# Diagonal inverses of a recurrence substituted in 16x16 blocks and joined to 32x32 by a level of small TensorE products

## The chip, the core and the metric

The kernel runs on one core of one Trainium2 chip. The metric is the device time of one execution in microseconds (us), the median of several runs. The engines are TensorE (PE in the profile; its weight loads are PEld), VectorE (DVE), ScalarE (ACT), GpSimd (POOL) and SyncE (SP), which issues DMAs here. A line such as L698 is a line of the kernel before; the lines of the changed kernel stand higher, by 4 ahead of the changed functions and by 33 behind them (L698 becomes L731).

## What is computed

One inference step of a one-layer decoder trunk over 576 tokens (a prompt of 512 and 8 samples of 8 tokens), width 1024. A combined projection feeds two head groups; their outputs go through an output projection, a SwiGLU and a gated embedding. The change lies in the second group, 16 heads of width 64 whose state follows a delta rule:

```python
def step(s, inp):
    r_t, w_t, k_t, v_t, kk_t, a_t = inp
    s_kk = jnp.einsum('bhvk,bhk->bhv', s, kk_t)
    s = (s * w_t[:, :, None, :] - s_kk[..., None] * (kk_t * a_t)[:, :, None, :]
         + v_t[..., None] * k_t[:, :, None, :])
    return s, jnp.einsum('bhvk,bhk->bhv', s, r_t)
```

The kernel takes it in chunks of 64 tokens. Inside a chunk the steps depend on each other through a triangular 64x64 matrix I + L for each head, and the kernel needs its inverse. There are 9 chunks (8 of the prompt, one holding the samples), 16 heads.

## The kernel before

**Fills.** The projections run as `fill`s: one fill makes 128 columns of the projection for all 576 tokens, as 48 TensorE products of 128x288 (L221, L222, L223 in `mm3`; an input and a weight are each split into two parts, and three of the four products are made). Weights are loaded (`raw`), rounded on ScalarE (`whi`, through the helper at L93) and their rest taken on GpSimd or VectorE (`wlo`, L206). The program calls a stated number of fills at stated places (`fill_at`, `fill_for`), and a scheduler then sets the order on each engine, within what tiles and pools allow. In what follows "a fill" as a count is one such TensorE product.

**Quarters.** The 16 heads go in four quarters of four heads (q = 0 to 3; two pairs jj of two heads e). For a quarter: its projections (`fill_for`), `prep` (decays, normalised keys, scaled operands), `start_states`, `gram` (L613, the products between tokens of a chunk, masked into `Lst`, which holds L), `bonus` (L246) and `decayed`; then `inverse`, which is `solve`, some fills, and `combine`; then `chain` and `head_norm`.

**solve (L652).** A 64x64 matrix is taken as 2x2 blocks of 32. The two diagonal blocks (z = 0, 1) of all heads and chunks are 72 blocks of 32x32, which four DMAs and a load bring to 72 partitions, one block to each (`L`). VectorE starts from I - L and runs 30 steps of substitution on whole blocks: step jx multiplies (L674) and subtracts (L676) jx·(31 - jx) elements in each partition. A transposed copy of the 36 blocks with z = 0 (L677) overwrites L. Td (the inverses) and Ad (the transposed ones) go to DRAM.

**combine (L681).** Td and Ad are loaded into `TT` and `AA`, block by block to the partitions e·64 + z·32. Then 32 products of 32x32 (L698; each is two instructions in the trace) into one PSUM tile, an eviction with the sign turned (L705 on VectorE and a ScalarE one), 32 more products (L712) and an eviction (L719 and ScalarE) that puts the off-diagonal blocks into TT.

**chain (L739).** Steps 1, then the samples (0), then 2 to 8, each step over TensorE, ScalarE and VectorE: L789, an eviction `xs` (L792), the product with the inverse (L797), L802, an eviction (L805), L823 and the state's update (L831), and L812 beside it. `marks` only notes instructions for other places.

**What orders the work here.** The PSUM pool `cx` (two tiles, taken in turn) serves combine, chain and head_norm, so a quarter's combine starts its products behind the head norm of the quarter before. The chain of a quarter runs beside the preparation of the next one. For quarter 3, whose inverse is called late, the preparation of the other head group follows directly: a load of dt (L997, on SyncE's queue, behind the stores of head_norm, L917), a running sum on VectorE (L1020 to L1043), an exponential on ScalarE, and 15 transposes of 16 columns on TensorE (L1037).

## Time and profile before

| | |
|---|---|
| three runs | 1345.02, 1345.34, 1348.39 us; median 1345.34 |
| span of the profiled execution | 1349.0 us |
| mean granted TensorE clock | 0.940 |
| busy: PE, DVE, ACT, POOL | 1246.8, 826.0, 618.9, 625.6 us |
| L674 and L676 together, 240 operations | 94.4 us of VectorE |

The profile is of one execution, which is not one of the three runs. Busy times are sums over the whole span. The stretch from 146 to 600 us holds the inverses of the four quarters and the chains of the first three; ahead of it lie loading, the first projections and quarter 0's preparation, behind it quarter 3's chain beside the rest of the trunk. A granted clock of 1 is full speed.

### The profile page before, as it was taken

What the parts mean: (1) busy time and instruction counts of PE and PEld (TensorE: products, weight loads), DVE (VectorE), ACT (ScalarE), POOL (GpSimd) and SP (SyncE); (2) the same over time, 40 slices, a digit from 0 to 9 for tenths busy, and PEclk for the clock granted to TensorE, in tenths of its full rate; (3) what the DMA queues carried; (4) which work ended last, traced back from release to release, by engine and by line L of the source; (5) the groups of instructions that cost most, each with busy time, mean ns of one, the idle gap of its engine ahead of it and who ended that gap; (6) DMA issues with size and microseconds to landing.
All of it is one profiled execution on the core that took longest, in us unless ns stands there. A gap on an engine that the chain in (4) does not pass through costs nothing.

```text
span 1349.0 us, 26596 instructions
## 1 busy us (share of the span) xinstructions
PE 1246.8 (92%) x10525; PEld 1150.7 (85%) x10525; DVE 826.0 (61%) x1443; ACT 618.9 (46%) x1256; POOL 625.6 (46%) x597
## 2 busy tenths in 40 slices
PE   6897999999989978899999969989999999999997
PEld 6787897889868957788779859889999999999997
DVE  6648666887687785943466667886553135443454
ACT  6565436534654463343434364464442124433363
POOL 5425413642355154122456645565654336654642
PEclk9897799899979978889989989998999999999998
DMA  5322242234232412262454542222323222314322
GB/s 164 125 68 66 77 117 63 85 103 116 75 99 78 109 41 80 94 214 83 157 176 131 179 125 72 73 93 88 92 88 87 79 86 82 93 59 149 96 89 71
DMA packets 94461, 135.58 MB, mean 100 GB/s; under 512 B 34705, under 2 KB 39057, under 8 KB 94337
## 3 DMA queue, kind: packets, MB, share of 16 engines
q1 hardware_dynamic: 93760, 133.36, 32.4%
q8 instruction: 83, 1.36, 0.4%
q10 hardware_dynamic: 576, 0.52, 0.1%
q14 instruction: 42, 0.34, 0.1%
HBM read 106.10 MB, written 27.75 MB: 99 GB/s over the span
## 4 chain that ended last, share of the span: by engine, by line
PE 63%; DVE 14%; ACT 4%; issue 4%; DMA 3%; POOL 3%; DVEq 0%; SPq 0%; ACTq 0%; POOLq 0%
PE lin L234 21%; PE lin L1403 8%; PE lin L223 6%; PE lin L221 6%; PE lin L222 6%; DVE h L395 2%; PE lin L1508 1%; PE lin L1509 1%; PE lin L1510 1%; DVE tmp L674 1%; DVE wlo L206 1%; DVE Tt L676 1%; PE lin L613 1%; PE cx L797 1%; DVE suv L831 1%
## 5 line engine op out<-in xcount | busy, mean ns | idle before, releaser
L206 POOL TENSOR_TENSOR wlo<-raw,whi 128x512 fp32r<-128x512 f32 (+1 forms) x108 | 146.4, 1356 | 352.5 <-ACT whi L93 269.5
L93 ACT ACTIVATE whi<-raw 128x512 fp32r<-128x512 f32 (+1 forms) x232 | 143.3, 618 | 259.1 <-PE lin L234 126.4
L221 PE MATMUL lin<-xhi,whi 128*128 128x288 f32 (+1 forms) x784 | 243.3, 311 | 2.5 <-ACT whi L93 2.2
L223 PE MATMUL lin<-xhi,wlo 128*128 128x288 f32 (+1 forms) x784 | 241.5, 308 | 2.3 <-POOL wlo L206 2.3
L222 PE MATMUL lin<-xlo,whi 128*128 128x288 f32 (+1 forms) x784 | 241.5, 308 | 0.3 <-POOL xlo L194 0.3
L206 DVE TENSOR_TENSOR wlo<-raw,whi 128x512 fp32r<-128x512 f32 (+1 forms) x124 | 100.9, 814 | 103.2 <-PE lin L234 60.4
L221 PEld LDWEIGHTS lin<-xhi,whi 128*128 128x128 f32 (+1 forms) x784 | 151.0, 193 | 9.3 <-ACT whi L93 2.6
L223 PEld LDWEIGHTS lin<-xhi,wlo 128*128 128x128 f32 (+1 forms) x784 | 150.7, 192 | 6.2 <-POOL wlo L206 2.8
L222 PEld LDWEIGHTS lin<-xlo,whi 128*128 128x128 f32 (+1 forms) x784 | 150.8, 192 | 4.8 <-issue 1.2
L234 PE MATMUL lin<-xhi,whi 128*128 128x288 f32 x384 | 62.3, 297 | 3.2 <-ACT xhi L93 3.0
L234 PE MATMUL lin<-xlo,whi 128*128 128x288 f32 x384 | 60.8, 298 | 0.0
L234 PE MATMUL lin<-xhi,wlo 128*128 128x288 f32 x384 | 59.3, 297 | 0.0
L234 PEld LDWEIGHTS lin<-xhi,whi 128*128 128x128 f32 x384 | 54.6, 189 | 3.8 <-ACT xhi L93 1.7
L234 PEld LDWEIGHTS lin<-xlo,whi 128*128 128x128 f32 x384 | 54.8, 191 | 0.0
L234 PE MATMUL lin<-ah,wlo 128*128 128x288 f32 x352 | 54.7, 296 | 0.0
L234 PE MATMUL lin<-al,whi 128*128 128x288 f32 x352 | 54.7, 296 | 0.0
L234 PE MATMUL lin<-ah,whi 128*128 128x288 f32 x352 | 54.7, 296 | 0.0
L234 PEld LDWEIGHTS lin<-xhi,wlo 128*128 128x128 f32 x384 | 54.3, 191 | 0.0
L1403 PE MATMUL lin<-T,wh 128*128 128x288 f32 x320 | 50.1, 296 | 4.5 <-DVE T L194 2.8
L674 DVE TENSOR_TENSOR tmp<-L,Tt 72x30 f32<-72x30 f32 (+14 forms) x120 | 49.2, 410 | 3.2
L234 PEld LDWEIGHTS lin<-ah,whi 128*128 128x128 f32 x352 | 49.6, 189 | 0.0
L234 PEld LDWEIGHTS lin<-ah,wlo 128*128 128x128 f32 x352 | 49.6, 189 | 0.0
(425 smaller groups left out, 3197.8 us busy)
## 6 DMA issues: line engine op xcount, KB each, us to landing
raw<-wts SPq DMA_DIRECT2D x271, 256.0 KB, 2.6
S<-s_wkv SPq DMA_DIRECT2D x8, 512.0 KB, 5.1
hd<-s_ssm SPq DMA_DIRECT2D x8, 512.0 KB, 4.5
o_ssm_s<-hd SPq DMA_DIRECT2D x8, 512.0 KB, 2.9
xbc_d<-E SPq DMA_DIRECT2D x12, 288.0 KB, 2.1
x<-xT SPq DMA_DIRECT2D x8, 288.0 KB
gate_d<-g SPq DMA_DIRECT2D x8, 288.0 KB, 2.5
bv_d<-rw SPq DMA_DIRECT2D x8, 288.0 KB
```

Source lines behind the costliest of these rows:

```text
L93: return S.activation(out, in_, func, bias=bias, scale=scale)
L206: eng.tensor_tensor(lo[:, 0:n], raw[:, 0:n], hi[:, 0:n].bitcast(F32), ALU.subtract)
L221: T.matmul(ps[:, a:b], whi, xhi[:, a:b], start=first, stop=False)
L222: T.matmul(ps[:, a:b], whi, xlo[:, a:b], start=False, stop=False)
L223: T.matmul(ps[:, a:b], wlo, xhi[:, a:b], start=False, stop=last)
L234: T.matmul(ps[:, a:e], (hi, lo)[p][:, i * P:(i + 1) * P], xs[k + i][q][:, a:e], start=n == k + i == 0, stop=n == 2 and k + i == nk - 1, sk ...
L395: V.scalar_tensor_tensor(h[:], E[:, i:i + 600], w(i), h[:], ALU.mult, ALU.add)
L613: T.matmul(ps[:, c:c + 128].rearrange("p (a t) -> p a t", a=2), s.BK[jj][H[e], g].rearrange("p a t -> p (a t)"), s.G[H[e], g, jj, :, e], s ...
L674: V.tensor_tensor(o, L[:, jx:jx + 1, jx + 1:32].to_broadcast([NB, jx, n]), Tt[:, 0:jx, jx:jx + 1].to_broadcast([NB, jx, n]), ALU.mult)
L676: V.tensor_tensor(Tt[:, 0:jx, jx + 1:32], Tt[:, 0:jx, jx + 1:32], o, ALU.subtract)
L797: T.matmul(uw[H[e], jj, :], TT[H[e], g, jj, :], xs[H[e], jj, :], start=True, stop=True)
L1403: T.matmul(ps, (hi, lo)[p][:, k * P:(k + 1) * P], OPS[n][k][q], start=first and p == q == k == 0, stop=p == 1 and k == 3, skip_group_check ...
```

## The change

A diagonal block of 32x32 is now split once more, into two corners of 16x16 and an off-diagonal block of 16x16. VectorE substitutes both corners of all 72 blocks at once: 14 steps, step jx on 2·jx·(15 - jx) elements in each partition. `Tt` is one tile, cleared once at the start of the program, so the elements outside the corners stay zero; ScalarE writes the negated corners into it. The transposed copy is made by ScalarE, for all 72 blocks, so Ad is twice as long and four loads bring AA in place of two.

`combine` gets a level ahead of the old one. 64 products (L707) multiply L with the inverses' first corner in AA, in the four strips of 32 partitions, into one PSUM tile. VectorE evicts them with a factor per partition, `half`, which is -1 on the second 16 partitions of each 32 and 0 on the first. Then 64 products of 16x16 (L716) and 32 of 32x16 (L719, for z = 0 alone) into the two halves of another PSUM tile; VectorE adds the latter to AA (L723, two operations) and ScalarE copies the former into TT (L724, four copies). The old level follows as it was (L731, L745).

```diff
@@ -453,6 +453,10 @@
     H = (slice(0, 64), slice(64, 128))
     jj2 = (0, 1)
 
+    half = const("half", [P, 1])
+    V.tensor_reduce(half[:], ident[:].rearrange("p (q y k) -> p q y k", q=4, y=2)[:, :, 1, :], AX.XY, ALU.add, negate=True)
+    Tt = s2.tile([72, 1056], F32, tag="Tt", name=nm("Tt"))
+    G.memset(Tt[:], 0.0)
     inverses = []
     for i in range(2):
         TT = (se, sp)[i].tile([P, 9, 2, 64], F32, tag=f"TT{i}", name=f"TT{i}")
@@ -654,29 +658,34 @@
         q = s.q
         Ld = dp.tile([2, 2, 18, 32, 32], F32, tag=f"Ld{q}", name=f"Ld{q}")
         s.Td = dp.tile([2, 2, 18, 32, 32], F32, tag=f"Td{q}", name=f"Td{q}")
-        s.Ad = dp.tile([2, 18, 32, 32], F32, tag=f"Ad{q}", name=f"Ad{q}")
+        s.Ad = dp.tile([2, 2, 18, 32, 32], F32, tag=f"Ad{q}", name=f"Ad{q}")
         NB = 72
         for z in range(2):
             for e in range(2):
                 r0 = e * 64 + z * 32
                 nc.sync.dma_start(Ld[z, e].rearrange("g s t -> s g t"),
                                   s.Lst[r0:r0 + 32, :, :, z * 32:z * 32 + 32].rearrange("s g j t -> s (g j) t"))
-        L = sp.tile([NB, 32, 32], F32, tag="L", name=nm("L"))
-        nc.sync.dma_start(L[:], Ld[:].rearrange("z e g s t -> (z e g) s t"))
-        Tt = s2.tile([NB, 32, 32], F32, tag="Tt", name=nm("Tt"))
-        V.tensor_scalar(Tt[:], L[:], -1.0, None, ALU.mult)
-        V.tensor_tensor(Tt[:].rearrange("p s t -> p (s t)")[:, 0:1024:33],
-                        Tt[:].rearrange("p s t -> p (s t)")[:, 0:1024:33], ones[0:NB, 0:32], ALU.add)
-        tmp = s2.tile([NB, 256], F32, tag="tmp", name=nm("tmp"))
-        for jx in range(1, 31):
-            n = 31 - jx
-            o = tmp[:, 0:jx * n].rearrange("p (s t) -> p s t", s=jx)
-            V.tensor_tensor(o, L[:, jx:jx + 1, jx + 1:32].to_broadcast([NB, jx, n]),
-                            Tt[:, 0:jx, jx:jx + 1].to_broadcast([NB, jx, n]), ALU.mult)
-            V.tensor_tensor(Tt[:, 0:jx, jx + 1:32], Tt[:, 0:jx, jx + 1:32], o, ALU.subtract)
-        V.tensor_copy(L[0:36], Tt[0:36].rearrange("p s t -> p t s"))
-        nc.sync.dma_start(s.Td[:].rearrange("z e g s t -> (z e g) s t"), Tt[:])
-        nc.sync.dma_start(s.Ad[:].rearrange("e g s t -> (e g) s t"), L[0:36])
+        def whole(t):
+            return t[:, 0:1024].rearrange("p (s t) -> p s t", t=32)
+
+        def corners(t):
+            return t.rearrange("p (y c) -> p y c", y=2)[:, :, 0:512].rearrange("p y (s t) -> p y s t", t=32)
+
+        L = sp.tile([NB, 1056], F32, tag="L", name=nm("L"))
+        nc.sync.dma_start(L[:, 0:1024], Ld[:].rearrange("z e g s t -> (z e g) (s t)"))
+        Lc, Tc = corners(L[:]), corners(Tt[:])
+        act(Tc[:, :, 0:16, 0:16], Lc[:, :, 0:16, 0:16], scale=-1.0)
+        V.tensor_tensor(Tt[:, 0:1024:33], Tt[:, 0:1024:33], ones[0:NB, 0:32], ALU.add)
+        tmp = s2.tile([NB, 112], F32, tag="tmp", name=nm("tmp"))
+        for jx in range(1, 15):
+            n = 15 - jx
+            o = tmp[:, 0:2 * jx * n].rearrange("p (y s t) -> p y s t", y=2, s=jx)
+            V.tensor_tensor(o, Lc[:, :, jx:jx + 1, jx + 1:16].to_broadcast([NB, 2, jx, n]),
+                            Tc[:, :, 0:jx, jx:jx + 1].to_broadcast([NB, 2, jx, n]), ALU.mult)
+            V.tensor_tensor(Tc[:, :, 0:jx, jx + 1:16], Tc[:, :, 0:jx, jx + 1:16], o, ALU.subtract)
+        nc.sync.dma_start(s.Td[:].rearrange("z e g s t -> (z e g) (s t)"), Tt[:, 0:1024])
+        act(whole(L), whole(Tt).rearrange("p s t -> p t s"))
+        nc.sync.dma_start(s.Ad[:].rearrange("z e g s t -> (z e g) (s t)"), L[:, 0:1024])
 
     def combine(s):
 
@@ -687,8 +696,32 @@
                 r0 = e * 64 + z * 32
                 nc.sync.dma_start(TT[r0:r0 + 32, :, :, z * 32:z * 32 + 32].rearrange("s g j t -> s (g j) t"),
                                   s.Td[z, e].rearrange("g s t -> s g t"))
-            nc.sync.dma_start(AA[e * 64:e * 64 + 32].rearrange("s g j t -> s (g j) t"),
-                              s.Ad[e].rearrange("g s t -> s g t"))
+                nc.sync.dma_start(AA[r0:r0 + 32].rearrange("s g j t -> s (g j) t"),
+                                  s.Ad[z, e].rearrange("g s t -> s g t"))
+        quads = [(e * 64 + z * 32, z) for e in range(2) for z in range(2)]
+        Wp = cx_ps()
+        Wv = Wp[:, 0:256].rearrange("p (g j t) -> p g j t", g=8, j=2)
+        for g in range(1, 9):
+            for jj in jj2:
+                for r0, z in quads:
+                    T.matmul(Wv[r0:r0 + 32, g - 1, jj, :], s.Lst[r0:r0 + 32, g, jj, z * 32:z * 32 + 32],
+                             AA[r0:r0 + 32, g, jj, 0:16], start=True, stop=True)
+        Ws = s2.tile([P, 8, 2, 16], F32, tag="Ws", name=nm("Ws"))
+        V.tensor_scalar(Ws[:], Wv, half[:], None, ALU.mult)
+        Xp = cx_ps()
+        Xv, Xt = (Xp[:, c:c + 256].rearrange("p (g j t) -> p g j t", g=8, j=2) for c in (0, 256))
+        for g in range(1, 9):
+            for jj in jj2:
+                for r0, z in quads:
+                    T.matmul(Xv[r0:r0 + 16, g - 1, jj, :], Ws[r0:r0 + 32, g - 1, jj, :],
+                             TT[r0:r0 + 32, g, jj, z * 32 + 16:z * 32 + 32], start=True, stop=True)
+                    if z == 0:
+                        T.matmul(Xt[r0:r0 + 32, g - 1, jj, :], TT[r0:r0 + 32, g, jj, 0:32],
+                                 Ws[r0:r0 + 32, g - 1, jj, :], start=True, stop=True)
+        for r0, z in quads:
+            if z == 0:
+                V.tensor_tensor(AA[r0:r0 + 32, 1:9, :, 0:16], AA[r0:r0 + 32, 1:9, :, 0:16], Xt[r0:r0 + 32], ALU.add)
+            act(TT[r0:r0 + 16, 1:9, :, z * 32 + 16:z * 32 + 32], Xv[r0:r0 + 16])
         Wp = cx_ps()
         Wv = Wp[:].rearrange("p (g j t) -> p g j t", g=8, j=2)
         for g in range(1, 9):
```

On TensorE, this is the end of quarter 1's gram beside the chain of quarter 0, before (G and bk are the gram's, cx and suv the chain's, lo the bonus sums', whi a fill's weights):

```order
L613 MATMUL lin_464_3183<-G_389_2686,bk_443_2986 128x128 x2
L797 MATMUL cx_276_1902<-xs_275_1899,TT0_465 64x64 x4
L802 MATMUL cx_277_1907<-ar_137_981,suv_263_1837 64x64 x4
L769 MATMUL tr_289_1974<-ident_76,bk_169_1145 128x128
L769 MATMUL tr_289_1974<-ident_76,bk_192_1282 128x128
L246 MATMUL lin_465_3201<-lo_413_2822,blk_83 128x288 x2
L812 MATMUL cx_277_1907<-G_138_982,suv_263_1837 64x64
L823 MATMUL cx_281_1923<-suv_263_1837,bkt_273_1894 64x64 x4
L812 MATMUL cx_277_1907<-G_138_982,suv_263_1837 64x64 x3
L246 MATMUL lin_466_3207<-lo_436_2959,blk_83 128x288 x2
L221 MATMUL lin_573_3836<-xhi_34_350,whi_575_3839 128x288
```

and now:

```order
L617 MATMUL lin_467_3326<-G_392_2829,bk_446_3129 128x128 x2
L617 MATMUL lin_467_3326<-G_392_2829,bk_423_2992 128x128 x2
L617 MATMUL lin_467_3326<-G_392_2829,bk_446_3129 128x128 x2
L845 MATMUL cx_290_2096<-G_139_986,suv_282_2060 64x64
L856 MATMUL cx_291_2103<-suv_282_2060,bkt_286_2083 64x64 x4
L845 MATMUL cx_290_2096<-G_139_986,suv_282_2060 64x64 x3
L246 MATMUL lin_468_3344<-lo_416_2965,blk_83 128x288 x2
L822 MATMUL cx_294_2122<-suv_283_2063,G_139_986 128x128 x2
L246 MATMUL lin_469_3350<-lo_439_3102,blk_83 128x288 x2
L221 MATMUL lin_578_4118<-xhi_34_350,whi_580_4121 128x288
L222 MATMUL lin_578_4118<-xlo_35_351,whi_580_4121 128x288
```

Before, the product with the inverse that stands behind the last gram product is that of step 5; now step 6 is past it and the L822 is that of step 7. Ahead of the preparation the first step now stands among fills, where there was none.

On TensorE, at the joining of quarter 3 (cx on the left is the joining's, rxg the head norm's of quarter 2, ident a transpose):

```order
L523 MATMUL cx_828_5547<-ident_76,rxg_827_5545 128x128 x4
L526 MATMUL cx_829_5553<-ident_76,rxg_827_5545 128x128
L760 MATMUL tr_992_6735<-ident_76,rw_870_5893 128x128
L760 MATMUL tr_992_6735<-ident_76,rw_878_5961 128x128
L698 MATMUL cx_958_6545<-AA_957_6538,Lst_914_6153 32x32 x32
L221 MATMUL lin_1062_7097<-xhi_34_350,whi_1064_7100 128x288
L222 MATMUL lin_1062_7097<-xlo_35_351,whi_1064_7100 128x288
L223 MATMUL lin_1062_7097<-xhi_34_350,wlo_1065_7101 128x288
```

and now, from the last transposes of the other head group's preparation on:

```order
L1070 MATMUL cb_1086_7743<-ident_76,dt_929_6672 128x16
L1070 MATMUL cb_1086_7743<-ident_76,ac_1083_7733 128x16
L1070 MATMUL cb_1086_7743<-ident_76,smask_1080_7724 128x16
L731 MATMUL cx_967_7105<-AA_963_6926,Lst_921_6574 32x32 x32
L221 MATMUL lin_1071_7657<-xhi_34_350,whi_1073_7660 128x288
L222 MATMUL lin_1071_7657<-xlo_35_351,whi_1073_7660 128x288
L223 MATMUL lin_1071_7657<-xhi_34_350,wlo_1074_7661 128x288
```

The 32x32 products (L698) stood behind the head norm and two transposes. Now the new level's products stand there, then 15 of these transposes (L1070, dt, ac and smask in turn), and then the 32x32 products (L731).

On VectorE, the same place (AA, Ws and TT1 are the joining's; ac, al, smask, dr and r16 the other head group's), before:

```order
L705 TENSOR_SCALAR AA_957_6538<-cx_958_6545 32x512
L915 SCALAR_TENSOR_TENSOR yo_830_5557<-gb_818_5489,pv_69 128x576
L1014 TENSOR_TENSOR idr_1072_7168<-ident_76 128x16
L1020 TENSOR_SCALAR ac_1074_7173<-dt_922_6251,nega_73 16x576
L1021 SCALAR_TENSOR_TENSOR ac_1074_7173<-smask_1071_7164,ac_1074_7173 16x576
L1023 COPY al_1075_7176<-ac_1074_7173 16x4
L1024 COPY al_1075_7176<-ac_1074_7173 16x8
L1028 TENSOR_TENSOR smask_1071_7164<-al_1075_7176,ac_1074_7173 16x512
L1026 TENSOR_TENSOR smask_1071_7164<-al_1075_7176,ac_1074_7173 16x64
L1049 TENSOR_TENSOR dr_1079_7205<-ident_76,al_1075_7176 16x192
L1043 TENSOR_TENSOR r16_1078_7201<-ac_1074_7173,r16_1078_7201 16x576
L719 COPY TT1_467<-cx_959_6580 32x16x32
```

and now:

```order
L948 SCALAR_TENSOR_TENSOR yo_837_5978<-gb_825_5910,pv_69 128x576
L1047 TENSOR_TENSOR idr_1081_7728<-ident_76 128x16
L710 TENSOR_SCALAR Ws_965_7000<-cx_964_6935,half_465 128x256
L1053 TENSOR_SCALAR ac_1083_7733<-dt_929_6672,nega_73 16x576
L1054 SCALAR_TENSOR_TENSOR ac_1083_7733<-smask_1080_7724,ac_1083_7733 16x576
L1056 COPY al_1084_7736<-ac_1083_7733 16x4
L1057 COPY al_1084_7736<-ac_1083_7733 16x8
L1061 TENSOR_TENSOR smask_1080_7724<-al_1084_7736,ac_1083_7733 16x512
L1059 TENSOR_TENSOR smask_1080_7724<-al_1084_7736,ac_1083_7733 16x64
L1082 TENSOR_TENSOR dr_1088_7765<-ident_76,al_1084_7736 16x192
L1076 TENSOR_TENSOR r16_1087_7761<-ac_1083_7733,r16_1087_7761 16x576
L723 TENSOR_TENSOR AA_963_6926<-AA_963_6926,cx_966_7002 32x16x16 x2
```

The eviction of the old level stood ahead of the operations on dt. Now the eviction of the new level does, and the additions to AA, on which the old level waits, stand behind them.

## The prediction

> **What bounds the kernel now.** I read the page's first part, then one table of stretches cut where the trunk changes its work, then single instructions inside those stretches. The page first: span and busy time per engine.
>
> ```profile
> span 1349.0 us, 26596 instructions
> PE 1246.8 (92%) x10525; PEld 1150.7 (85%) x10525; DVE 826.0 (61%) x1443; ACT 618.9 (46%) x1256; POOL 625.6 (46%) x597
> ```
>
> TensorE (PE) is busy 92%, VectorE (DVE) 61%. That is an average; the change touches one part of the run. The table of stretches gives start and end, length, busy time of each engine with its instructions, TensorE's granted clock, DMA share and GB/s.
>
> ```profile
> 146.00:204.00 58.00, 56.66 (x521) 54.05 (x519) 42.37 (x96) 22.16 (x46) 12.09 (x13) 0.97 0.36 100
> 204.00:268.00 64.00, 58.73 (x545) 48.42 (x545) 47.04 (x83) 40.50 (x87) 33.30 (x45) 0.89 0.25 75
> 268.00:344.00 76.00, 73.51 (x682) 68.32 (x680) 60.01 (x140) 31.32 (x76) 27.59 (x31) 0.98 0.39 111
> 344.00:409.00 65.00, 59.52 (x608) 49.80 (x608) 50.37 (x84) 39.79 (x86) 31.02 (x42) 0.84 0.24 75
> 409.00:469.00 60.00, 57.08 (x481) 52.01 (x478) 45.29 (x117) 21.71 (x56) 19.02 (x20) 0.97 0.38 103
> 469.00:526.00 57.00, 44.93 (x562) 34.69 (x562) 40.66 (x77) 33.40 (x74) 24.93 (x30) 0.82 0.16 52
> 526.00:567.00 41.00, 36.27 (x318) 31.28 (x314) 33.54 (x86) 13.47 (x34) 12.05 (x13) 0.94 0.36 104
> 567.00:596.00 29.00, 25.47 (x267) 21.92 (x267) 15.68 (x36) 11.42 (x22) 5.62 (x8) 0.73 0.42 120
> 596.00:680.00 84.00, 82.44 (x715) 67.54 (x715) 35.13 (x88) 39.40 (x93) 30.03 (x27) 0.98 0.47 157
> ```
>
> Three kinds alternate. In 146–204, 268–344 and 409–469 TensorE runs projection products (the fills) without a pause, 56.66 of 58 us at a clock of 0.97; the substitutions of quarters 0, 1 and 2 lie under them on VectorE. In 204–268, 344–409 and 469–526 the next quarter is prepared beside the chain of this one, and no engine is full. In 526–567 quarter 3's substitution stands between the chain's own VectorE work: 33.54 of 41 us. From 596 TensorE is full again (82.44 of 84), so whatever delays it before that moves the end.
>
> **What the change does, part by part.**
>
> *Substitution.* The two operations of a step, over the whole run:
>
> ```profile
> L674 DVE TENSOR_TENSOR tmp<-L,Tt 72x30 f32<-72x30 f32 (+14 forms) x120 | 49.2, 410 | 3.2
> L676 DVE TENSOR_TENSOR Tt<-Tt,tmp 72x30 f32<-72x30 f32 (+14 forms) x120 | 45.2, 377 | 3.4
> 148.57 0.18 DVE L674 TENSOR_TENSOR tmp<-L,Tt 72x30 f32<-72x30 f32 x1
> 151.50 0.27 DVE L674 TENSOR_TENSOR tmp<-L,Tt 72x108 f32<-72x108 f32 x1
> ```
>
> Before: (49.2 + 45.2) / 4 = 23.6 us a quarter, 60 operations. After: 28 operations of 28 to 112 elements, between 0.18 and 0.27 us each, so about 6.5 us. Some 17 us of VectorE go from each quarter. Under the fills of quarters 0, 1 and 2 that shortens nothing as long as TensorE is full. Only its pauses can go, and one pause there belongs to the inverse: the joining products waited for their operand. Row of the waits in 146 to 196 (total, times, longest):
>
> ```profile
> PE cx L698 <- DMA AA<-Ad: 1.3, 1, 1.3
> ```
>
> I take −1.3 for it. The same table of stretches bounds it: TensorE's idle time in the three full stretches is 1.3 + 2.5 + 2.9 = 6.7 us, so no more than −6.7. If VectorE were the bound there, the same edit would be worth up to 17 us a quarter.
>
> *What else is added.* ScalarE gets the negation, a transposed copy of all 72 blocks that waits for the last substitution, and four small copies a quarter; VectorE loses its copy. Behind the copy on ScalarE are roundings of weights for fills (L93). Their weights come tiles ahead and ScalarE is busy 22 of 58 us in such a stretch, so I cost it at nothing, at most the 1.07 us of VectorE's own copy (row further down) if a fill waits behind it. The second half of Ad and two more AA loads are two more issues on SyncE; DMA is at 0.36 there: nothing, as the quarter's inverse is not awaited there any more. The cleared tile and the row of factors are made once at the start: nothing, bounded by a fraction of a microsecond.
>
> *Small products.* The nearest row is the old joining of 32x32 blocks:
>
> ```profile
> 194.66 1.19 PE L698 MATMUL cx<-AA,Lst 32*32 32x32 f32 x62
> ```
>
> 62 instructions in 1.19 us are 19.2 ns each; each product is two instructions, and they alternate between two row strips, so one strip takes one every 38.4 ns. The new level has 64 products on four strips, and 96 of which the two strips with z = 0 have 32 each: 16 × 2 × 38.4 ns = 1.2 us, and 32 × 2 × 38.4 = 2.5 us, 3.7 us a quarter if four strips run abreast. If no more overlaps than in that row, it is 320 × 19.2 ns = 6.1 us; if a 16-wide product is quicker, less, down to half, 1.9. I take 3.7, as the width of one strip is what the row measures. In quarters 0 and 1 this lies in full stretches: **+7.4** (3.7 to 12.3). [...]
>
> *Steps of the chain.* The joining comes earlier, so the chain does too. By the order on TensorE, one step of quarter 0 (the first) now lies among the fills ahead of the next preparation; and behind the products of the next gram two steps are left instead of three (quarter 0) and two instead of three (quarter 1). Net, one step leaves the full stretches. What a step costs TensorE there:
>
> ```profile
> 204.66 0.45 PE L797 MATMUL cx<-xs,TT 64*64 64x64 f32 x8
> 204.94 0.40 PE L802 MATMUL cx<-ar,suv 64*64 64x64 f32 x8
> 209.61 0.45 PE L823 MATMUL cx<-suv,bkt 128*64 128x64 f32 x8
> 209.89 0.40 PE L812 MATMUL cx<-G,suv 128*64 128x64 f32 x6
> 510.05 0.71 PE L789 MATMUL cx<-suv,G 128*128 128x128 f32 x4
> 515.50 0.61 PE L789 MATMUL cx<-suv,G 128*128 128x128 f32 x4
> ```
>
> By starts 0.28 + 0.40 + 0.28 + 0.40 + 0.61 = 2.0 us: **−2.0**. The last two rows are consecutive steps with little between them: 5.45 us, what a bare step costs in latency.
>
> *Preparation stretches 204–268 and 344–409.* They hold as many steps as before or one more. TensorE idles 5.3 and 5.5 us in them. Ends: one bare step shorter each if the chain ends them (−10.9), one longer in one of them (+5.5). I take 0, since nothing that the preparation itself waits for is changed: VectorE there had no substitution.
>
> *Quarter 2's joining in 469–526.* The head start lets it begin before the preparation, but its end stands behind it. One more round over the shared PSUM tiles is: products, an eviction, products, an eviction. An eviction of 32x32 blocks, from quarter 3:
>
> ```profile
> 590.40 0.68 DVE L705 TENSOR_SCALAR AA<-cx 32x512 f32<-32x512 f32 x1 [1.04 <-PE cx L698]
> ```
>
> With 3.7 us of products and two such evictions that is 5.1 us if it is bare; TensorE idles 12 us in this stretch. 0 to +5.1, I take **+2**.
>
> *Quarter 3's substitution, 526–574.* Rows of the stretch 526–567, and of the transposed copy behind it with what waited:
>
> ```profile
> L676 DVE TENSOR_TENSOR Tt<-Tt,tmp 72x184 f32<-72x184 f32 (+14 forms) x23 | 9.8, 425 | 0.7
> L674 DVE TENSOR_TENSOR tmp<-L,Tt 72x168 f32<-72x168 f32 (+14 forms) x24 | 9.2, 385 | 0.7
> 573.31 1.07 DVE L677 COPY L<-Tt 36x1024 f32<-36x1024 f32 x1
> 574.31 0.44 DVE L902 COPY ar<-cx 128x288 f32<-128x288 f32 x1
> 593.37 0.29 PE L222 MATMUL lin<-xlo,whi 128*128 128x288 f32 x1
> 593.50 0.29 PE L223 MATMUL lin<-xhi,wlo 128*128 128x288 f32 x1
> L246 PE MATMUL lin<-lo,blk 128*128 128x288 f32 x8 | 2.5, 432 | 0.7 <-DVE G L631 0.7
> ```
>
> 19 us of VectorE shrink to some 7. But TensorE is next: 144 fills at 0.13 us (the two single fills, start to start) are 18.7, two steps and the rest of a third among them 5.0, and two bare steps at the end 10.9: by the order four steps stand behind gram 3 now, against three. With 2.5 us of bonus sums (L246) that is 37.1 of the 41 us, −3.9. The copy moves to ScalarE, so the head norm's copy behind it starts about 1.0 us earlier (−4.9 with both). The products of a step wait for each other on TensorE's queue, so I take **−4.0**, between −10 (all of VectorE's 12 us, less what is left of it beside fills) and 0.
>
> *Quarter 3's joining.* Here the joining is bare, and the order puts it behind something else. The rows of before:
>
> ```profile
> 588.43 1.92 PE L698 MATMUL cx<-AA,Lst 32*32 32x32 f32 x64
> 590.93 0.44 PE L223 MATMUL lin<-xhi,wlo 128*128 128x288 f32 x1
> 591.17 0.44 PE L221 MATMUL lin<-xhi,whi 128*128 128x288 f32 x1
> 592.33 0.42 SPq L997 DMA_DIRECT2D dt<-dt_d  x1
> 594.37 0.51 DVE L1020 TENSOR_SCALAR ac<-dt,nega 16x576 f32<-16x576 f32 x1 [2.35 <-DMA dt<-dt_d]
> 594.65 1.20 PE L712 MATMUL cx<-TT,AA 32*32 32x32 f32 x64
> 597.47 0.69 ACT L93 ACTIVATE smask<-smask 16x576 f32<-16x576 f32 x1 [0.36 <-DVE smask L1026]
> 599.75 0.33 PE L797 MATMUL cx<-xs,TT 64*64 64x64 f32 x2
> ```
>
> Before, the 32x32 products start at 588.43, at once behind the head norm; fills follow, the second products at 594.65, and the first product with the joined inverse (L797) at 599.75. After, the new level's products stand first, then 15 transposes (L1070) that read dt, its running sum and its exponential, and only then the 32x32 products. The load of dt is issued 3.9 us behind the head norm (588.43 to 592.33), since it is queued behind the head norm's stores; its exponential ends at 598.16. So the new level (3.7 us and its evictions) is hidden in that wait, and the 32x32 products start near 599, 10.5 us later than now. Part comes back: fills between the two sets of products ran at 0.24 us at first (590.93 to 591.17) and could run at 0.13 (22 fills, 2.4 us). About +8; VectorE's adds and ScalarE's four copies wait in the same queues, so it can reach +10; if dt came earlier against the head norm, it would be 0. I take **+7**.
>
> The sum: 7.4 − 1.3 − 2.0 + 0 + 2 − 4.0 + 7 = +9.1 against the profiled execution's span of 1349.0, so 1358.1. That execution is 3.7 us above the median of the runs, 1345.34. The forecast is 1358.1 − 3.7 = 1354.4, I say **1354.5**. What a measurement of this kernel can tell from no change is about 0.3%, 4 us: under 1341.3 is faster, over 1349.4 is slower.
>
> **Rivals.**
>
> *Strips take turns.* If the products of four strips into one PSUM tile exclude each other, they keep the row's 19.2 ns: 6.1 us a quarter, the sum 2 × 2.4 = 4.8 us higher, 1359.3. [...] For it: nothing shows four strips. Against it: two strips into one tile run at 19.2 ns an instruction, but that row cannot say what one alone takes. Chance 0.10.
>
> *No change.* The wait for dt costs nothing, as its load is early enough or its transposes find time elsewhere: 7.4 − 1.3 − 2 + 2 − 4 = +2.1, 1347.4. Against it is the store ahead of the load. Chance 0.20.
>
> *Faster.* The chain, not the preparation, ends the stretches 204–268 and 344–409. From the point where the gram of quarter 1 ends one step sooner than now, each gives back 5.45 us; with quarter 3's stretch at −8 and the dt wait at +4: 7.4 − 1.3 − 2 − 10.9 + 0 − 8 + 4 = −10.8, 1334.5. For it: VectorE works 47 and 50 us in these stretches and the chain passes through it at every step. Against it: the preparation keeps its place in the order. Chance 0.28.
>
> **How the numbers follow.** The forecast's own case has 0.42 and holds 1349.5 to 1363; with the strips' case slower has 0.52, same 0.20, faster 0.28. The range takes the faster case down to 1333 and the upper ends (both strips' and quarter 3's) to 1365; what is left out is half of the faster case's lower tail and a little above, under 0.2.
>
> **What would show it.** Right: stretches of quarters 0 and 1 longer by the new products at near 20 ns or less; the L1070 transposes waiting for ScalarE's exponential with the 32x32 products of quarter 3 behind them, about 10 us after the head norm. Wrong: gram of quarter 1 ending over 4 us earlier against the start of its preparation; quarter 3's chain ending over 8 us sooner; the 32x32 products of quarter 3 starting less than 4 us behind the head norm; or new products above 40 ns each.

## The result and the profile after

The changed kernel takes 1380.49 us (median of four runs, 1376.38 to 1392.16), against 1346.59 for the kernel before: a ratio of 1.0272, 95% interval 1.0234 to 1.0311; the medians differ by 33.9 us. The forecast was 1354.5, at most 1365. The direction held, the size did not. Its profiled execution has a span of 1374.7 us, 25.7 over the 1349.0 of before, and is the fastest of its four runs; where the two spans differ is what the traces can show.

The page of the changed kernel, span and busy time:

```profile
span 1374.7 us, 29062 instructions
PE 1259.6 (92%) x11805; PEld 1162.4 (85%) x11805; DVE 768.7 (56%) x1320; ACT 632.7 (46%) x1278; POOL 620.7 (45%) x598
```

VectorE lost 57 us and TensorE is busy 13 us longer with 1280 more instructions (640 products), yet the span grew by 25.7. The place is found by the same fill product in both traces: the fills are the same 5472 products in nearly the same order, so the start of the n-th one is a clock (worked out from the starts of L221, L222, L223 and L234). Up to quarter 3 a chain step may stand on the other side of such a point, so single differences mix; from 2209 on all work before it is the same.

| start of fill product | what follows | before | after | without the level |
|---|---|---|---|---|
| 769 | first products of quarter 0's joining, after | 170.1 | 168.0 | 167.6 |
| 984 | preparation of quarter 1 | 204.0 | 211.6 | 212.4 |
| 1437 | quarter 1's joining, after | 325.9 | 329.7 | 332.7 |
| 1553 | preparation of quarter 2 | 346.7 | 360.1 | 359.5 |
| 1705 | behind gram 2 | 413.8 | 425.1 | 418.6 |
| 2017 | behind gram 3 | 532.5 | 545.3 | 524.6 |
| 2207 | end of quarter 2's head norm | 581.8 | 597.4 | 565.0 |
| 2209 | behind quarter 3's first 32x32 products | 590.3 | 616.9 | 572.8 |
| 3400 | output projection | 884.6 | 912.1 | 863.7 |

(The last column is an experiment, below.) Quarter 0's joining starts 2 us earlier; from there to the preparation of quarter 1 nearly 10 us are lost, and 10 again around quarter 1's joining. These losses are not the level's by themselves: the kernel without it is as late at 984 and at 1553, since in both some chain steps now stand ahead of these points. The two part behind 1553. Counted by the product with the inverse, at 1994 the kernel before and the changed one have done 18 chain steps and the one without the level 20, at nearly the same time as the changed one (478.7 and 478.5 us); at 2207 all three have done 27. In all 15.6 us are lost before quarter 3's joining, which adds 11 more; behind it nothing changes.

Quarter 0's first new products, and where quarter 1's second ones stand (start, duration, engine, line, count):

```profile
172.37 1.21 PE L707 MATMUL cx<-AA,Lst 32*32 32x16 f32 x122
...
335.87 0.21 PE L719 MATMUL cx<-Ws,TT 32*32 32x16 f32 x3
339.15 0.23 PE L716 MATMUL cx<-TT,Ws 32*16 32x16 f32 x8 [3.08 <-issue]
339.61 0.40 PE L222 MATMUL lin<-xlo,whi 128*128 128x288 f32 x1
339.85 0.30 PE L223 MATMUL lin<-xhi,wlo 128*128 128x288 f32 x1
340.12 0.29 PE L222 MATMUL lin<-xlo,whi 128*128 128x288 f32 x1
340.41 0.44 PE L221 MATMUL lin<-xhi,whi 128*128 128x288 f32 x1
340.65 0.44 PE L222 MATMUL lin<-xlo,whi 128*128 128x288 f32 x1
```

122 instructions in 1.21 us: four strips into one PSUM tile run abreast at 10 ns an instruction. It is the strips more than the narrower products: from start to start two strips of 32 columns take 16.4 ns (L698, quarter 0), four of 32 columns 10.2 (the run with half as many of twice the width, below), four of 16 columns 8.5 (L707). But in the middle of the second burst TensorE stands 3.08 us for nothing that the profile shows ("issue"), and of the fills behind it the ones from 340.41 on start 0.24 us apart where they had been 0.13: half the clock (0.50 is granted from 340.4 to 343.7 us). In the waits of TensorE from 146 to 690 the entry of this pause (three in all) is the largest, and before has none like it:

```profile
PE cx L716 <- issue: 5.2, 3, 3.1
PE tr L802 <- ACT bkt L93: 3.3, 2, 3.0
```

Quarter 3's joining, on the chain of waits of the changed kernel:

```profile
603.69 1.92 POOL gb L946
...
606.85 2.42 DMA dt<-dt_d
...
609.90 1.36 DVE ac L1054
...
612.59 0.75 DVE r L1076
...
613.37 0.42 DVE AA L723
...
613.81 0.37 ACT TT L93
...
614.62 0.43 DVE AA L723
...
615.09 1.91 PE cx L731 x62
617.00 0.54 PE lin L221
617.54 0.24 PE lin L222
```

This is the wait that the prediction named: the load of dt, its sum, r16, then the additions to AA, then the 32x32 products (L731), 12 us behind the head norm. The granted clock (the number behind the busy times) over 18 us from there on, in the changed kernel, the kernel before and the one without the level:

```profile
603.00:621.00 18.00, 13.10 (x420) 12.34 (x419) 8.58 (x19) 4.78 (x10) 3.49 (x6) 0.53 0.72 251
```
```profile
588.00:606.00 18.00, 17.87 (x240) 16.34 (x239) 9.92 (x21) 6.78 (x14) 4.26 (x7) 0.86 0.79 277
```
```profile
571.00:589.00 18.00, 18.00 (x256) 16.65 (x257) 10.19 (x22) 7.71 (x15) 4.27 (x7) 0.91 0.82 294
```

TensorE idles 4.9 us of the 18 and has 0.53 of its clock, where before it had 0.86.

### The profile page after: what moved, and what is told of

Same layout as the page of the kernel before. It is cut to its first block, busy times and chain, and to the rows that moved or that the text cites. A ratio compares the mean times of both kernels' runs of the same rounds, so it can differ in the third digit from the quotient of the medians.

```text
span 1374.7 us, 29062 instructions
## 1 busy us (share of the span) xinstructions
PE 1259.6 (92%) x11805; PEld 1162.4 (85%) x11805; DVE 768.7 (56%) x1320; ACT 632.7 (46%) x1278; POOL 620.7 (45%) x598
## 4 chain that ended last, share of the span: by engine, by line
PE 43%; DVE 6%; ACT 2%; DMA 2%; issue 2%; POOL 1%; DVEq 0%; SPq 0%; ACTq 0%; POOLq 0%
PE lin L234 21%; PE lin L1436 7%; PE lin L221 2%; PE lin L222 2%; PE lin L223 2%; DMA raw<-wts 1%; PE lin L1541 1%; DVE T L194 1%; PE lin L1542 1%; DVE xlo L1336 1%; PE y L1237 1%; PE d L1186 1%; PE lin L1543 1%; PE d L1198 1%; DVE xs L1249 0%
## 5 line engine op out<-in xcount | busy, mean ns | idle before, releaser
L221 PE MATMUL lin<-xhi,whi 128*128 128x288 f32 (+1 forms) x784 | 244.1, 312 | 7.0 <-ACT whi L93 4.0
L223 PE MATMUL lin<-xhi,wlo 128*128 128x288 f32 (+1 forms) x784 | 240.3, 307 | 3.2 <-DVE wlo L206 2.0
L222 PE MATMUL lin<-xlo,whi 128*128 128x288 f32 (+1 forms) x784 | 241.6, 308 | 0.0
L221 PEld LDWEIGHTS lin<-xhi,whi 128*128 128x128 f32 (+1 forms) x784 | 150.2, 192 | 15.4 <-ACT whi L93 5.1
L223 PEld LDWEIGHTS lin<-xhi,wlo 128*128 128x128 f32 (+1 forms) x784 | 150.0, 192 | 8.3 <-DVE wlo L206 2.8
L222 PEld LDWEIGHTS lin<-xlo,whi 128*128 128x128 f32 (+1 forms) x784 | 150.5, 192 | 5.0 <-issue 1.7
L234 PE MATMUL lin<-xhi,whi 128*128 128x288 f32 x384 | 62.2, 297 | 3.3 <-ACT xhi L93 3.0
L234 PE MATMUL lin<-xlo,whi 128*128 128x288 f32 x384 | 60.8, 298 | 0.0
L234 PE MATMUL lin<-xhi,wlo 128*128 128x288 f32 x384 | 59.2, 297 | 0.0
L234 PEld LDWEIGHTS lin<-xhi,whi 128*128 128x128 f32 x384 | 54.5, 189 | 3.8 <-ACT xhi L93 1.8
L234 PEld LDWEIGHTS lin<-xlo,whi 128*128 128x128 f32 x384 | 54.8, 191 | 0.0
L234 PE MATMUL lin<-ah,whi 128*128 128x288 f32 x352 | 54.7, 296 | 0.0
L234 PE MATMUL lin<-ah,wlo 128*128 128x288 f32 x352 | 54.7, 296 | 0.0
L234 PE MATMUL lin<-al,whi 128*128 128x288 f32 x352 | 54.7, 296 | 0.0
L234 PEld LDWEIGHTS lin<-xhi,wlo 128*128 128x128 f32 x384 | 54.2, 190 | 0.0
L234 PEld LDWEIGHTS lin<-ah,whi 128*128 128x128 f32 x352 | 49.6, 189 | 0.0
L234 PEld LDWEIGHTS lin<-ah,wlo 128*128 128x128 f32 x352 | 49.6, 189 | 0.0
L234 PEld LDWEIGHTS lin<-al,whi 128*128 128x128 f32 x352 | 49.6, 189 | 0.0
```

Source lines behind the costliest of these rows:

```text
L221: T.matmul(ps[:, a:b], whi, xhi[:, a:b], start=first, stop=False)
L222: T.matmul(ps[:, a:b], whi, xlo[:, a:b], start=False, stop=False)
L223: T.matmul(ps[:, a:b], wlo, xhi[:, a:b], start=False, stop=last)
L234: T.matmul(ps[:, a:e], (hi, lo)[p][:, i * P:(i + 1) * P], xs[k + i][q][:, a:e], start=n == k + i == 0, stop=n == 2 and k + i == nk - 1, sk ...
```

## The experiments

Theory A is the prediction's: TensorE's own time in the full stretches, and quarter 3's wait for dt. Its first rival, B, is the new path of the substitution; further theories came as these fell.

**Quarter 3's pause filled.** One mark moves the fills ahead of the second-level products.

```diff
-    places = [("n", 2), ("c", 3), ...
+    places = [("n", 2), ("x", 3), ...   # x: the last L716 product
```

> The changed kernel with one mark moved: the last fills ahead of quarter 3's chain are queued on TensorE behind the new level's products, where they were queued behind the 32x32 products. Theory A (the change loses in quarter 3's joining since TensorE has nothing to do while VectorE works through dt, its sum and its exponential, 11 us there): the pause is filled, the span goes from 1374.7 to about 1364 and the ratio to the kernel before from 1.027 to about 1.018. Theory B (what is lost is lost by the substitution's new path, ScalarE's transposed copy, the doubled Ad and its loads): within 3 us of the changed kernel.

Measured 1.0242, 1.0198 to 1.0287. Between fill products 2207 and 2255 the loss against before is 5.6 us (from 18.6 to 24.2) where it was 11.3; about half came back there. The whole gained 4 us, less than its interval, where A had 11.

**dt behind the joining.** The third part of the other head group's preparation is queued behind L723, the ScalarE copies and L731.

> The changed kernel with the operations on dt queued behind quarter 3's joining on VectorE, ScalarE and TensorE, so that the 32x32 products no longer wait for dt. Theory A: the 32x32 products start at most 7 us behind the head norm where it is 12 now, TensorE pauses only for the new level's own evictions, and the time falls by 5 to 9 us, the ratio to about 1.021. Theory B: within 3 us of the changed kernel.

Measured 1.0259, 1.0220 to 1.0298. The 32x32 products wait no longer for dt. This run is 3.4 us later than the changed kernel when the level starts, so the two are compared from there: from the level's first product (L707) to the bulk of the 32x32 products it takes 8.5 us (606.80 to 615.28) where it took 11.7 (603.41 to 615.09). The chain of waits there:

```profile
609.02 0.82 DVE yo L948
609.84 0.41 DVE Ws L710
...
611.86 0.19 issue
612.05 0.18 PE cx L719
613.57 0.42 DVE AA L723
614.01 0.37 ACT TT L93
614.40 0.38 ACT TT L93
614.81 0.43 DVE AA L723
```

The new level stands there by itself: its eviction behind yo on VectorE, its products, then four operations on the same PSUM tile one after the other; behind it 33 of the 32x32 instructions take 1.11 us where 64 of L745 later take 1.13, and fills stand 0.24 us apart: half the clock. dt was the last to arrive in the changed kernel, but it accounts for 3.2 of the 11.7 us only; the level without it takes 8.5. A had at most 7.

**Without the level.**

```diff
-        (L707 products, L710, L716 and L719 products, L723, four copies)
```

> The changed kernel without the new level: no products of 16 columns, no eviction of them, nothing added to AA and nothing copied into TT, so the off-diagonal 16x16 blocks are left out of the inverses; the substitution, its ScalarE copy and the loads stay as changed. Theory A (the level's products, their waits and what they delay make the loss, and VectorE's relief gives little): 0.994 to 1.002 of the kernel before. Theory B: still over 1.012.

Measured 0.9916, 0.9889 to 0.9944: B falls, the level costs 47 us (1380 less 1333). The ratio lies just under A's range. Without it the change would win 11.

**VectorE's relief alone.** 28 operations in place of 60, in the kernel before.

> The kernel before with VectorE's 60 operations of a substitution cut to the 28 of the changed kernel, so the off-diagonal 16x16 blocks come out wrong; copy, loads and joining are as before. It measures VectorE's relief alone. Theory A (TensorE bounds the three full stretches and quarter 3's chain is bound by its own latency): 0.994 to 1.000 of the kernel before. The rival that the relief is worth its VectorE time in quarter 3 and a step in each preparation: 0.985 or less.

Measured 1.0028, 1.0006 to 1.0051: no gain at all, with VectorE busy 763.9 us in place of 826.0. Its trace is ahead for a while: at fill product 2209 it stands at 581.8 us where the kernel before stands at 590.3, and it loses these 8.5 us again behind, 5.4 of them between fill products 2500 and 2600 and 4.2 more behind the last one. Why is not shown. That this run and the one without the level differ by 15 us, though both substitute alike, is taken up under the copies on ScalarE.

**A delay alone, the products alone.** Theory C, formed here, says that joining, chain, head norm and next joining have no slack, so the level's latency is paid in full.

```diff
+        one = AA[:, 1, 0, 0:1]
+        for _ in range(18):
+            V.tensor_scalar(one, one, 1.0, None, ALU.mult)
+            act(one, one)
```

> The kernel without the new level (third run), with a delay ahead of the 32x32 products in its place: 36 operations of one element each, in turn on VectorE and ScalarE, each waiting for the other, on an element that the first product reads. No TensorE work is added. Theory C (joining, chain, head norm and the next joining follow each other without slack through all four quarters, so what a joining takes longer is paid in full, wherever TensorE is full of fills): with d the time that the delay takes in the trace, the kernel is about 4 d slower than the third run, which was at 0.9916; for d of 8 to 12 us that is 1.015 to 1.028. Theory A (TensorE's own time in the full stretches is what counts there, and only quarter 3 is bare): at most d and some, 0.995 to 1.003.

Measured 1.0069, 1.0041 to 1.0098. First operation of the delay and first 32x32 product in quarter 1:

```profile
306.47 0.15 DVE L703 TENSOR_SCALAR AA<-AA 128x1 f32<-128x1 f32 x1 [2.33 <-DMA AA<-Ad]
...
329.08 0.50 PE L711 MATMUL cx<-AA,Lst 32*32 32x32 f32 x20
```

The 36 operations took 11 to 15 us a quarter, and from the first of them to the first product it is 14 to 23 us in the first three quarters (in the fourth they ran before `cx` was free). The kernel became 21 us slower than the run without the level, less than half of the operations' time. C falls as put, and A's range, which ends at 1.003, was too low.

> The kernel without the new level (third run), with the level's 160 products issued behind each joining: same shapes, reading AA and L, writing a PSUM tile that nothing reads; no evictions and nobody waits for them. It adds the level's TensorE time and not its latency. Theory C: about 3.7 us a quarter at most, 0.992 to 1.002. Theory A: the level is paid by TensorE time, so this alone should bring back most of the 47 us between the changed kernel and the third run: over 1.010.

Measured 1.0267, 1.0222 to 1.0311. The products with nobody waiting for their result bring back all 47 us. This was against C; A had over 1.010, though by its price of own time alone they would cost 15. TensorE's waits in this run, on the second burst:

```profile
PE cx L743 <- issue: 5.8, 3, 2.1
PE cx L743 <- ACT TT L93: 5.6, 3, 5.1
```

The second line is a limit of this run: the products themselves wait for the eviction of the `cx` tile that they write (5.1 us in quarter 3), and they take both `cx` tiles, which the chain uses next.

From fill product 600 to 2600, TensorE's time from one start to the next, by what stood there (pause: what goes beyond 0.13 us where the next start is over 0.5 us away; in brackets the fills that start while the granted clock is one half; worked out from the trace):

| us | before | without the level | products alone | after |
|---|---|---|---|---|
| level's products | | | 16.6 | 15.8 |
| 32x32 products | 10.8 | 10.1 | 9.5 | 12.0 |
| fills (number at half clock) | 299.2 (85) | 298.3 (58) | 310.2 (145) | 303.3 (112) |
| other products | 199.8 | 198.1 | 205.7 | 202.2 |
| pauses | 77.5 | 63.6 | 78.0 | 84.2 |
| sum | 587.4 | 570.0 | 620.0 | 617.5 |

The products themselves take 4 us a quarter, as forecast. In the run with the products alone twice that comes with them, as pauses and as other work at a lower clock. In the changed kernel the level's products and 20.6 us of pauses make most of the 47.5 us over the run without the level; some 6 of these 20.6 are pauses in or just behind the bursts for which the profile shows no releaser, the rest are waits for other engines, quarter 3's among them.

**The new level on the old substitution.**

> The new level without the shorter substitution: VectorE does the 30 steps on whole 32x32 blocks as before, ScalarE copies, and the new level's products and evictions follow although their result is then counted twice in the off-diagonal blocks. Theory C: the level's latency is paid in full and nothing is saved ahead of it, 1.030 to 1.045. Theory A: like the changed kernel, 1.020 to 1.030.

Measured 1.0476, 1.0437 to 1.0515, 61 us slower than before and above both ranges. The shorter substitution gives back 25 of these, though alone it gave nothing, which suggests that what it is worth depends on what waits for the joining.

**Copies on ScalarE.**

> The kernel before with the negation and the transposed copy of 36 blocks moved to ScalarE, the substitution and the joining as before. It asks what of the gain of the third run (0.9916) over the fourth (1.0028), which share the short substitution, is ScalarE's. Theory C: the copy lies between the last substitution and the joining, so about 1 us a quarter, 0.994 to 0.999. If the difference between those two runs was only a different order of other work: 0.999 to 1.005.

Measured 1.0092, 1.0058 to 1.0125, slower by 11 us: neither expectation. With the 15 us between the two short substitutions it suggests that the order which the scheduler finds after a small edit moves this kernel by 10 to 15 us either way, so that the price of an edit needs more than one base. For the two short substitutions the traces don't bear this out: they set their chain steps among nearly the same fills (quarter 0's first step at fill product 833 and 834). Where those 15 us come from stays open.

**How the cost grows.** Theory D, a guess behind the pauses of 3.08 us in the changed kernel and 2.1 us in the run with the products alone: a burst that is too long stops ("runs dry"), a short one costs its time. That TensorE lacks instructions then, as the name says, no run shows.

> The run with the products alone (1.0267), with every second chunk's products left out: 80 products a quarter, 160 instructions, which the order now sets as two bursts of 64 and 96 instructions with fills between. Theory D (a product costs about 10 ns as long as TensorE has instructions at hand; a burst that is longer than some 150 to 200 small instructions runs dry, stands 2 to 5 us, and the fills behind it run at half the clock): no burst runs dry, so 0.995 to 1.004. Theory E (each product costs its share, half of them half of the 47 us): 1.007 to 1.012.

> The run with the products alone, with all 160 products of a quarter, but set in eight groups of 20 products (40 instructions), one behind each step of the chain. Theory D: no group runs dry and each costs 0.4 to 0.5 us and its entry, 14 to 18 us in all and partly in pauses of TensorE, 0.996 to 1.006. Theory E: as much as in one burst, 1.020 to 1.030.

> The run with the products alone, with 80 products a quarter of 32 columns in place of 160 of 16: the same columns, half the instructions. Theory D: like the run with half of the products, within 0.004 of it. If the columns or the width of the strips make the cost: 1.020 to 1.030.

> The changed kernel with the new level's 160 products replaced by three wide ones (128x256) that write the same PSUM tiles, so the blocks come out wrong; its evictions, additions and copies stay, and so does every wait between them. With the products alone it splits the 47 us between the changed kernel and the one without the level. Theory D with the delay's run (57 us of delay cost 20 us): the level's evictions and waits are some 5 us of latency a quarter, a third of it paid, so 0.993 to 1.003. Theory C (latency in full): 1.006 to 1.015.

Measured: half of the products 1.0104 (1.0077 to 1.0131); spread over the chain 1.0395 (1.0367 to 1.0424); half as many of twice the width 1.0087 (1.0063 to 1.0110); evictions and waits alone 0.9973 (0.9946 to 1.0000). The evictions cost 8 us over the run without the level, as D had it. The number of instructions counts here, not the columns, as D had it too: with half as many the ratio is 1.0104 at 16 columns and 1.0087 at 32, against 1.0267 for all 160 of 16. But half cost half, as E had it, and spread they cost more than either had. Their order does not let them speak clearly: the run with half of them starts the chains of the first three quarters 17 to 85 fills later than the run without the level, and the spread groups stand between the chain's steps, each one on the path of the next step. And a short burst can stop too: in the run with half of them TensorE stands 3.05 us in quarter 3, 86 instructions into a burst of 96.

**The same products where no chain waits.** So the products were taken out of the chain's part: 640 of the same shapes, on constants, in the output projection of the kernel before.

```diff
     def scaled(c, g):
         ps = lin_ps()
+        if g == 1 and c % 2:            # second run: every c and g, 40 products each
+            (160 products as in the level, into ps)
         linear(...)
```

> The kernel before with four bursts of 160 small products (the new level's shapes, on constants, read by nothing) set ahead of four of the output projection's later tiles, where TensorE is full and no chain waits. It measures what the products cost on TensorE alone. Theory F (a product costs its own time plus the dry stall of its burst and the half clock behind it): 4 times 7 to 10 us, 1.020 to 1.030. Theory A's price (own time alone, 3.7 us a burst): 1.008 to 1.013. If the 47 us are paid only through the chain: under 1.013 too.

> As the run before, with the 640 products as 16 groups of 40 ahead of all 16 of those tiles. Theory F (stall and half clock come from a burst's length): 1.010 to 1.016. If each small product costs as much wherever it stands: as the run with four bursts.

Measured 1.0267 (1.0227 to 1.0308) for four bursts and 1.0107 (1.0076 to 1.0139) for sixteen groups: 36 us and 14 us for the same 640 products, both as F had it. 14 us are 22 ns a product, its own time (a group of 80 instructions takes 0.84 us). The stretches around the first burst, and what TensorE waited for in the stretch of the bursts, 838 to 893 us (total, times, longest):

```profile
820.00:838.00 18.00, 18.00 (x167) 17.82 (x167) 11.46 (x14) 6.64 (x11) 10.96 (x7) 1.00 0.27 74
838.00:850.00 12.00, 8.36 (x341) 8.00 (x340) 2.18 (x3) 1.98 (x3) 2.07 (x2) 0.67 0.16 48
850.00:855.00 5.00, 5.00 (x32) 5.00 (x31) 2.03 (x3) 1.00 (x2) 0.00 (x0) 0.76 0.06 5
```
```profile
PE lin L1328 <- issue: 4.3, 2, 2.2
PE lin L1332 <- issue: 3.9, 2, 2.4
PE lin L1334 <- issue: 3.9, 2, 2.3
```

And in the run with groups, the stretch of its last eleven groups, 828 to 872 us, where TensorE has no such wait:

```profile
828.00:872.00 44.00, 44.00 (x1128) 41.91 (x1128) 22.20 (x30) 14.38 (x25) 18.83 (x12) 1.00 0.23 63
```

A full stretch at clock 1.00 drops to 8.36 of 12 us busy and 0.67. A burst of 320 instructions lasts 5.5 to 8.0 us, of which 2.4 to 4.3 are one or two pauses, and the 15 to 25 fills behind it cost 1.6 to 2.9 us more than at full clock: 9 us a burst. In groups of 80 instructions between wide products such pauses are gone (44.00 of 44 us busy from 828 to 872).

Where pauses over 1.2 us stand within a burst, counted in its product instructions from where no fill or other product stands between them (worked out from the starts; each has a weight load of its own beside it):

| run | burst | pause behind instruction | us |
|---|---|---|---|
| four bursts | first | 171, 299 | 2.25, 1.77 |
| four bursts | second | 187, 315 | 2.60, 1.73 |
| four bursts | third, fourth | 202; 218 | 2.38; 2.52 |
| products alone | quarter 1 | 135, 263 | 2.07, 1.99 |
| products alone | quarter 2 | 67, 195 | 1.30, 2.27 |
| after | quarters 1, 2 | 155; 172 | 3.25; 2.06 |

Where a burst has two, they are 128 product instructions (64 products) apart, each time: 256 instructions with the weight loads. And the first is no accident of the burst. Counted from the program's start over all of TensorE's records (products, weight loads, the waits of its queue on semaphores), the product behind the pause has 193 or 194 records more than a multiple of 256 ahead of it, in all 28 such pauses without a releaser, of the nine runs that have any. So in these runs the pause goes by a place in the instruction stream, not by the length of the burst.

How long it lasts mostly goes with the time since the last such place. In the four bursts the 256 instructions up to a pause took 1.1 to 1.7 us, and with the pause 3.4 to 3.8. In the run with groups small products pass such a place eight times, without a pause: there the 256 instructions took 4.4 us and more, as fills stand among them. It is no fixed time: in quarter 3 of the run with half of the products a pause came after 3.9 us, and three times a place was passed after 1.5 us without one.

**On the other base.**

> The kernel before with the 160 products of a quarter behind each joining, read by nothing, and all else unchanged: the same addition as in the run with the products alone, on the other base. Theory F: the same cost of 40 to 50 us, 1.028 to 1.038. If the run without the level owed its 0.9916 to a lucky order that any addition destroys, the products' own cost is less: 1.012 to 1.022.

Measured 1.0366, 1.0321 to 1.0410: 47 us again, so the base did not make the cost. It is 12 us a quarter where a bare burst costs 9; what the other 3 are, the chain's delay, the `cx` tiles that the products take, or the order, stays open.

## Why the prediction was wrong

*Small products in quarters 0 and 1, +7.4.* This term failed. Their own time was sized well: 15.8 us in four quarters, 4 a quarter against 3.7. What failed is the step from there to the sum, that a product in a full stretch costs its own time. The run with products alone and the one in the output projection show 9 to 12 us a burst: TensorE nearly always stands still at one place of every 256 instructions where small products bring it there within 1.1 to 1.7 us, and the fills behind run at half clock (145 of the 2000 fills of the table, where without the level it is 58). The term was also made for two quarters; all four pay.

The rival of the strips that take turns is refuted: 122 instructions in 1.21 us, and a pair of strips more brings 32-column products from 16.4 to 10.2 ns. The small products' term left the clock out. In the changed kernel fills at 0.24 us follow the pauses of 3.25 and 2.06 us within the bursts of quarters 1 and 2, at a granted clock of 0.50 (340.4 to 343.7 and 487.2 to 490.4 us). In its quarter 0, whose pauses without a releaser stay under 1.1 us, the clock stays at 1.00 (166 to 200 us), so the small products alone don't halve it there. Why TensorE stands still at one place of every 256 instructions, with products and weight loads that start every 5 ns, no run shows.

*Steps of the chain, −2.0.* The steps were miscounted. By the trace of the changed kernel two steps of quarter 0 and one of quarter 1 now stand ahead of the next preparation (fill products 984 and 1538), where it took one. With two behind each gram in place of three the full stretches gain a step and do not lose one, so by the term's own price, an estimate, it should have been +2.0.

*VectorE's relief, −1.3 and −4.0.* The relief alone measured +0.3%, so taking nothing for the full stretches was right in the end. The −4.0 in quarter 3's stretch did not come in the changed kernel: between fill products 2017 and 2207 it lost 2.9 us more. With the relief alone 8.5 us were gained by fill product 2209, but not kept. The rival "faster", with a step gained in each preparation, is refuted as a forecast of the time by the same run.

*Quarter 2's joining, +2.* Between fill products 1994 and 2017 the loss grew by 5.7 us; the bound was 5.1. At 2017 the changed kernel has done one chain step less than before, so this and the 2.9 us behind it are best taken together: +8.6 where the two terms have −2.0. It is the largest miss of the sum. The head start that the shorter substitution gives had gone by then: without the level two steps more are done at 1994.

*Quarter 3's joining, +7.* It was 11, and the chain shows the wait for dt, named ahead. But the level was not hidden in that wait: with dt out of the way it takes 8.5 us by itself of the 11.7, where 3.7 and its evictions were put, and the run saved 2 us, less than its interval. And the part that was to come back, fills at 0.13 in place of 0.24, went the other way: in the stretch with the longer pause (603 to 621 us, 4.9 of them idle) the clock is 0.53, where it was 0.86.

The terms of the full stretches (small products, relief, steps), together +4.1, measured 7.7 from fill product 600 to 1994; quarters 2 and 3 make up the rest, 5.7, 2.9 and 11.1, of a total of 27.4 at fill product 2209. So the changed kernel's own trace does not put 9 us on each burst of the first two quarters; that price comes from the experiments, and in the changed kernel part of it may show later, as steps that are still to be done. At the end the spans differ by 25.7, the timed medians by 33.9. These 8 us lie in which executions were profiled: with the 1.7 us by which a run's time exceeds its span, that of the kernel before lies 4 us above its median and that of the changed kernel 4 below. The changed kernel's runs spread from 1376.38 to 1392.16 with mean granted clocks from 0.940 down to 0.925; why they spread so is open.

No version with the whole inverse beat the kernel before. Only the one without the level did (0.9916), which leaves blocks out; even with the level's products as good as free (evictions alone, 0.9973) the gain is within what a measurement can tell.

## What to carry to other kernels

Price small TensorE products by their number and by what stands between them, not by their columns: 160 in one burst cost 9 us here, in groups of 40 between wide products 3.6; and 80 of 32 columns a quarter came to a ratio of 1.0087, 160 of 16 to 1.0267. Where 256 TensorE instructions, weight loads counted, took 4.4 us or more, no pause without a releaser there was over 0.8 us; where they took under 2, there was nearly always one, of 0.9 to 3.4. If small products are needed, set them in small groups between wide products that do not wait for them, or fewer and wider. And what an engine off the bound is relieved of can't be counted on to pay for them: 62 us less of VectorE measured as no gain.

## What was not expected of the hardware

Four row strips into one PSUM tile run at 10 ns an instruction (two: 19.2). Long runs of small products stopped, mostly for 1.3 to 3.4 us and with no releaser in the profile; where a burst had two stops, in four bursts, they were 128 product instructions apart, and all 28 stops in nine runs stood at the same place of a grid of 256 instructions counted from the program's start. The fills behind ran at half clock, 0.24 us apart in place of 0.13. Groups of 40 products between wide ones didn't stop (eleven groups at a clock of 1.00, 44.00 of 44 us busy): the same 640 cost 14 us so and 36 in bursts.
